# Gate_up in sections of two weight tiles, the scatter's halves between them, in a routed-expert loop

## The chip, the cores and the metric

One core of a Trainium2 chip runs the whole kernel. The metric is the device time of one execution in microseconds; lower is better. Before the change the median of 3 runs is 1408.82 us (1407.81 to 1412.9).

## What is computed

One encoder layer over 256 tokens of width 1024 in float32: an input projection feeds three mixers (latent attention, a Mamba-2 scan, a convolution module), gates merge them, an output projection and a layer norm follow. Then comes the part that matters here, a mixture of 32 experts with 4 experts per token, and a second layer norm:

```python
logits = (t @ router_w + router_b).astype(jnp.float32)
top_vals, top_idx = lax.top_k(logits, TOP_K)
gates = jax.nn.softmax(top_vals, axis=-1).astype(t.dtype)
...
h = xe @ w_gu[e] + b_gu[e]
gate, up = h[:, :D_FF], h[:, D_FF:]
gate = jnp.minimum(gate, SWIGLU_LIMIT)
up = jnp.clip(up, -SWIGLU_LIMIT, SWIGLU_LIMIT)
return ((up + 1) * (gate * jax.nn.sigmoid(SWIGLU_ALPHA * gate))) @ w_dn[e] + b_dn[e]
```

Each expert's rows are weighted by their gates and added to their tokens.

## The kernel before, in words

The program goes through the 32 experts in a fixed order. Each has 12 weight tiles of 1 MB (128 partitions by 2048 floats): tiles 0 to 7 are gate_up, each one slice of 128 of the 1024 inputs, tiles 8 to 11 are down. SP issues a load per tile, in order, into a ring of 19 slots; `load` waits until PE has read the slot's former tile for the last time. The first 19 tiles are loaded during the mixers.

How many tokens an expert has is known only at run time, so its code has conditional sections, entered or skipped by each engine. With up to 32 tokens (`size` 0) `up_four` runs: four matmuls for a tile, on four groups of 32 columns. With 33 to 64 (`size` 1) `up_many` runs instead, for 64 tokens. With 65 to 96 (`size` 2) both run, the first 64 tokens in one and the rest in the other. The down projection has the same two kinds of section. The router puts 84, 68 and 72 tokens on experts 2, 15 and 17; experts 3, 6, 7, 10, 12, 18, 24, 25, 30 and 31 have 33 to 64, all others no more than 32. No expert has over 96; for such experts there is an overflow loop, `heavy`, placed before expert 31 and guarded by one comparison of the largest count on PE, ACT, DVE and POOL. It is skipped here.

An expert's result is weighted (`weigh`, on ACT and DVE: yh, then yl) into tiles that all experts share (`parked`: sc, yh, yl). It is added to the tokens one expert later, by `flush(prev)`: for each half c of the tokens four matmuls (L1150) scatter it into two PSUM banks, and DVE adds both banks to the accumulator (L1154). The tag `sm` has two banks in all, so the second half's matmuls wait for the first half's adds. PE's order is the order in which the code is written. In `expert` it is: the sections of tiles 0 to 3, `flush(prev)`, then `aux` (the slots of the tokens and their gates, L1236 and L1097), then the sections of tiles 4 to 7, and then `fill` (part of a later expert's gather) and the down projection. Expert 31 is special: since `heavy` writes into `parked`, the scatter of expert 30 is done before the guard of the overflow loop.

The lines that the change touches:

```python
        for k0 in (0, KT // 2):
            with tc.If(pe > 0):
                up_many(k0)
            with tc.If(pe != 1):
                up_four(k0)
            if k0 == 0:
                flush(prev)
                aux = bank(5, f"aux{e}", [P, S + 2])
```

Of the kernel before, what the change touches and what calls it, by code (L numbers as in the profile page):

```python
# [10 lines left out]
F32R = mybir.dt.float32r  # L11
# [7 lines left out]
P = 128  # L19
D = 1024  # L20
S = 256
KT = D // P
# [155 lines left out]
def tile_trunk(ctx, tc, xT_d, xn_d, wf_d, vec_d, row_d, rw_d, cst_d, cst2_d, rope_d, ln1_d, ln2_d,  # L178
               bgu_d, bdn_d, wgu_d, wdn_d, out_d):
    nc = tc.nc  # L180
    V, A, T, PO = nc.vector, nc.scalar, nc.tensor, nc.gpsimd
# [539 lines left out]
    def load(e, u, n=None, eng=nc.sync):  # L721

        if (e, u) in pre:
            return pre.pop((e, u))
        t = ring_tile(f"{e}_{u}", n)
        if u < 8:
            eng.dma_start(t, wgu_v[e, u])
        else:
            t = t.rearrange("p (k n) -> p k n", k=2)
            eng.dma_start(t, wdn_v[e, (u - 8) // 2, u % 2])  # L730
        return t
# [424 lines left out]
    def flush(prev, cs=(0, 1)):  # L1156
        if prev:
            e, sc, yh, yl = prev
            for c in cs:
                pos = [sm(f"pos{e}{c}{n}") for n in range(2)]  # L1160
                scatter(pos, c, sc, (yh, yl))
                for n in range(2):
                    add(c, n, pos[n])
# [9 lines left out]
    def expert(e, oh, xg, bl, wt, prev, cur, fill):  # L1173
# [34 lines left out]
        def up_many(k0):  # L1208
            if k0 == 0:
                for q in range(2):  # L1210
                    T.matmul(pL[q], bl, bgu_t[:, q * 512:(q + 1) * 512], start=True, stop=False)
            for k in range(k0, k0 + KT // 2):
                for q in range(2):
                    for h in range(2):
                        T.matmul(pL[q][h * 64:(h + 1) * 64].rearrange("p (g n) -> p g n", g=2),  # L1215
                                 xg[:, k, s_], quarter(wt[k], h, q), start=False, stop=(k == KT - 1))

        def up_four(k0):
            if k0 == 0:
                for g, (h, q) in enumerate(QUARTERS):  # L1220
                    T.matmul(grp(pS, g), bl[:, g * TINY:(g + 1) * TINY].bitcast(F32),  # L1221
                             bgu_t[:, q * 512:(q + 1) * 512].bitcast(F32), start=True, stop=False)
            for k in range(k0, k0 + KT // 2):
                for g, (h, q) in enumerate(QUARTERS):
                    T.matmul(grp(pS, g).rearrange("p (g n) -> p g n", g=2), xs_[:, k],  # L1225
                             quarter(wt[k], h, q), start=False, stop=(k == KT - 1))

        for k0 in (0, KT // 2):
            with tc.If(pe > 0):
                up_many(k0)  # L1230
            with tc.If(pe != 1):
                up_four(k0)
            if k0 == 0:
                flush(prev)
                aux = bank(5, f"aux{e}", [P, S + 2])
                T.matmul(aux[:, 0:S], idr[:, e:e + 1].to_broadcast([P, P]), rankT, start=True, stop=True)  # L1236
                gate_mm(aux[:, S:S + 1], lambda c: oh[:, c, e % 2], e)
                gate_mm(aux[:, S + 1:S + 2], lambda c: ohs[:, c], e)
                gsl = ex.tile([P, 2], F32, tag="gsl", name=f"gsl{e}", bufs=4)
                V.tensor_copy(gsl, aux[:, S:S + 2])  # L1240
# [125 lines left out]
    prev = None  # L1366
    for e in range(NE):
        more = e // 2 + 1 < NE // 2
        if e % 2 == 0:
            oh, xg = ohn, xgn  # L1370
            if more:
                ohn = mo.tile([P, 2, 2, CAP], F32R, tag="ohp", name=f"ohp{e + 2}", bufs=2)
                xgn = mo.tile([P, KT, P], F32, tag="xg", name=f"xg{e + 2}", bufs=2)
                with tc.issue_after(last["ch"].ins):
                    for c in range(2):
                        onehot(ohn, c, e + 2)

        def fill(arm="", e=e, more=more):
            if more and e % 2 == 0:
                pg = [sm(f"pgx{e}{arm}{hf}") for hf in range(2)]  # L1380
                for c in range(2):
                    gather(pg, c, pair(ohn, c))
                A.copy(raw[:, 0:512], pg[0])
                V.tensor_copy(raw[:, 512:D], pg[1])
            elif more:
                spread_rows(xgn, rowk, f"{e}{arm}")

        wt = [load(e, u) for u in range(12)]
        bl = nbl
        if e + 1 < NE:  # L1390
            nbl = bias_lhs(e + 1)
        if e == NE - 1:

            flush(prev)
            prev = None
            free = [nload[0] + i for i in range(4)]
            with tc.If(count(NE, ALL) > TOP, label="overflow"):
                for x in range(NE):
                    with tc.If(count(x, ALL) > TOP):
                        for part in range(2):  # L1400
                            heavy(x, part, [load(x, u, free[u % 4], PO) for u in range(12)], (f"{x}x", *parked))
        cur = (e, *parked)
        with pe_order():
            expert(e, oh, xg, bl, wt, prev, cur, fill)
        prev = cur
# [153 lines left out]
```

## Time and profile before

| what | value |
|---|---|
| median of 3 runs | 1408.82 us |
| the profiled execution's own time | 1414.25 us |
| its span, first to last instruction | 1412.4 us |
| PE busy | 1169.7 us (83%) |
| DVE busy | 614.1 us (43%) |
| ACT busy | 328.1 us (23%) |
| transfers over the span | 322 GB/s on average |
| mean granted TensorE clock | 0.902 |
| matmul records of L1225 (`up_four`) and L1215 (`up_many`) | 1408 and 832 |

A section over one tile leaves 8 records, so 64 records are one expert: 22 experts ran `up_four` and 13 ran `up_many`. The mixers fill the span up to about 400 us, the experts take nearly all the rest, the last layer norm some 20 us. PE's share is an average over both parts; a matmul's end is modelled, so a busy PE may still be waiting in part. PEclk is the share of full clock that TensorE was granted. In a timeline row, the text in brackets is the idle time of the engine before the row and what ended it; a name with a q, as PEq, is an engine's sequencer, at the line of the section that it passed.

### The profile page before, as it was taken

What the parts mean: (1) busy time and instruction counts of PE and PEld (TensorE: products, weight loads), DVE (VectorE), ACT (ScalarE), POOL (GpSimd) and SP (SyncE); (2) the same over time, 40 slices, a digit from 0 to 9 for tenths busy, and PEclk for the clock granted to TensorE, in tenths of its full rate; (3) what the DMA queues carried; (4) which work ended last, traced back from release to release, by engine and by line L of the source; (5) the groups of instructions that cost most, each with busy time, mean ns of one, the idle gap of its engine ahead of it and who ended that gap; (6) DMA issues with size and microseconds to landing.
All of it is one profiled execution on the core that took longest, in us unless ns stands there. A gap on an engine that the chain in (4) does not pass through costs nothing. (4 is left out here: it accounts for less than half of the span.)

```text
span 1412.4 us, 20889 instructions
## 1 busy us (share of the span) xinstructions
PE 1169.7 (83%) x7635; PEld 620.8 (44%) x7635; DVE 614.1 (43%) x1245; ACT 328.1 (23%) x668; POOL 293.4 (21%) x293
## 2 busy tenths in 40 slices
PE   7797797899957987887888879898888888877875
PEld 7786687799822433233232324242322323212222
DVE  5999996877653233223323221323233322222213
ACT  5565563545421011101110010111001011000001
POOL 5999999543030000000000000000000000000000
PEclk9898888899968899999998998999989999987897
DMA  7342333467949878999999999997999999999991
GB/s 249 106 149 100 109 135 135 149 211 268 328 170 416 328 308 349 414 416 415 417 414 415 415 414 418 416 416 281 384 416 414 414 416 416 416 416 415 414 396 45
DMA packets 89496, 456.39 MB, mean 323 GB/s; under 512 B 8304, under 2 KB 8704, under 8 KB 58496
## 3 DMA queue, kind: packets, MB, share of 16 engines
q1 hardware_dynamic: 89344, 454.33, 81.3%
q8 instruction: 99, 1.62, 0.5%
q14 instruction: 53, 0.43, 0.1%
HBM read 453.25 MB, written 1.05 MB: 322 GB/s over the span
## 5 line engine op out<-in xcount | busy, mean ns | idle before, releaser
L1225 PE MATMUL pGS<-ew,xsm 128*32 128x512 f32 x1408 | 194.8, 694 | 23.8 <-DMA ew<-in_wgu_dram 12.1
L1448 POOL TENSOR_TENSOR xn<-xn,lb 128x256 f32<-128x256 f32 x4 | 2.8, 723 | 993.3 <-DVE xn L1436 993.3
L1215 PE MATMUL pGL<-ew,xg 128*64 128x512 f32 x832 | 203.3, 642 | 2.8 <-DMA ew<-in_wgu_dram 2.8
L1154 DVE TENSOR_TENSOR xn<-xn,pos 128x512 f32<-128x512 f32 x124 | 79.9, 684 | 221.2 <-PE pos L1150 218.8
L1143 DVE SCALAR_TENSOR_TENSOR yl<-pY,gsl,yh 128x512 fp32r<-128x512 f32 x35 | 26.3, 751 | 236.0 <-ACTq L1202 93.0
L1087 ACT ACTIVATE sg<-gv 128x256 f32<-128x256 f32 x48 | 20.0, 417 | 459.1 <-DVE gv L1086 458.3
L388 POOL TENSOR_TENSOR cbc<-cbc,ups 128x256 f32<-128x256 f32 x120 | 124.4, 1036 | 4.6
L1215 PEld LDWEIGHTS pGL<-ew,xg 128*64 128x64 f32 x832 | 66.2, 147 | 123.5 <-issue 112.1
L1225 PEld LDWEIGHTS pGS<-ew,xsm 128*32 128x32 f32 x1408 | 55.2, 123 | 141.9 <-issue 110.6
L243 DVE TENSOR_TENSOR wl<-raw,wh 128x1024 fp32r<-128x1024 f32 (+1 forms) x72 | 98.9, 1382 | 38.4 <-ACT wh L242 38.0
L1296 PE MATMUL pY<-ew,hT 128*32 128x512 f32 x704 | 91.3, 664 | 23.2 <-ACT hT L1282 21.9
L242 ACT CAST wh<-raw 128x1024 fp32r<-128x1024 f32 (+1 forms) x89 | 90.9, 1030 | 61.5 <-DMA raw<-in_wf_dram 20.5
L1265 PE MATMUL pY<-ew,hT 128*64 128x512 f32 x416 | 101.2, 643 | 0.0
L387 POOL TENSOR_TENSOR ups<-ups,vec 128x256 f32<-128x256 f32 x120 | 100.6, 857 | 0.0
L1150 PE MATMUL pos<-yh,sc 64*128 64x512 f32 x124 | 47.7, 513 | 31.9 <-DVE xn L1154 24.1
L1142 ACT ACTIVATE yh<-pY,gsl 128x512 fp32r<-128x512 f32 x35 | 24.1, 687 | 191.9 <-PE pY L1265 87.5
L1265 PEld LDWEIGHTS pY<-ew,hT 128*64 128x64 f32 x416 | 30.9, 147 | 61.5 <-issue 60.0
L1296 PEld LDWEIGHTS pY<-ew,hT 128*32 128x32 f32 x704 | 22.2, 120 | 77.7 <-issue 44.2
L1150 PEld LDWEIGHTS pos<-yh,sc 64*128 64x128 f32 x124 | 18.0, 189 | 83.5 <-DVE xn L1154 50.7
L1086 DVE TENSOR_SCALAR gv<-pGS 128x256 f32<-128x256 f32 x22 | 9.3, 425 | 103.7 <-PE pGS L1225 103.7
L1221 PE MATMUL pGS<-bgu_t,bl 128*32 128x512 f32 x176 | 24.3, 622 | 35.5 <-DVEq L1202 13.5
L243 POOL TENSOR_TENSOR wl<-raw,wh 128x1024 fp32r<-128x1024 f32 x17 | 41.6, 2451 | 52.6 <-ACT wh L242 52.6
(446 smaller groups left out, 2182.7 us busy)
## 6 DMA issues: line engine op xcount, KB each, us to landing
ew<-in_wgu_dram SPq DMA_DIRECT2D x241, 1024.0 KB, 19.9
ew<-in_wdn_dram SPq DMA_DIRECT2D x124, 1024.0 KB, 20.0
raw<-in_wf_dram SPq DMA_DIRECT2D x87, 512.0 KB, 3.9
ew<-in_wgu_dram SPq DMA_DIRECT2D x30, 512.0 KB, 7.0
ew<-in_wdn_dram SPq DMA_DIRECT2D x8, 512.0 KB, 5.2
xraw<-in_xT_dram SPq DMA_DIRECT2D x4, 256.0 KB, 5.4
xn<-in_xn_dram SPq DMA_DIRECT2D x2, 512.0 KB, 6.5
lnt<-in_ln_dram SPq DMA_DIRECT2D x2, 512.0 KB, 10.1
```

The source lines that it names most:

```text
L242: A.copy(h[:, b], raw[:, b])
L243: (PO if u in LOW_POOL else V).tensor_sub(l[:, b], raw[:, b], h[:, b].bitcast(F32))
L387: PO.tensor_tensor(pr, up[:, j:j + S], W("cw31", c * 31 + j).to_broadcast([P, S]), op=ALU.mult)
L388: PO.tensor_add(acc, acc, pr)
L1143: V.scalar_tensor_tensor(yl, pY, gsl, yh.bitcast(F32), op0=ALU.mult, op1=ALU.subtract)
L1150: T.matmul(pos[n], sc[r, c * P:(c + 1) * P], y[r], start=(start and i == 0), stop=(i == 1))
L1154: V.tensor_add(dst, dst, po)
L1215: T.matmul(pL[q][h * 64:(h + 1) * 64].rearrange("p (g n) -> p g n", g=2), xg[:, k, s_], quarter(wt[k], h, q), start=False, stop=(k == KT - 1))
L1221: T.matmul(grp(pS, g), bl[:, g * TINY:(g + 1) * TINY].bitcast(F32), bgu_t[:, q * 512:(q + 1) * 512].bitcast(F32), start=True, stop=False)
L1225: T.matmul(grp(pS, g).rearrange("p (g n) -> p g n", g=2), xs_[:, k], quarter(wt[k], h, q), start=False, stop=(k == KT - 1))
L1265: T.matmul(pY[0][n * 64:(n + 1) * 64], hT[b][:, j, h * CAP:(h + 1) * CAP], wt[KT + 2 * b + h][:, j, n * 512:(n + 1) * 512], start=False, s ...
L1296: T.matmul(grp(pY, 2 * n + j), hT[:, j, g * TINY:(g + 1) * TINY], w[:, j, n * 512:(n + 1) * 512], start=(j == 1 and (b, h) == (0, 0)), sto ...
```

## The change

The gate_up part runs in four pairs of sections of two tiles each instead of two pairs of four. The two halves of the scatter come after the first and the second pair, `aux` after the third. Before expert 31 the overflow loop no longer uses `parked`: it takes tiles of its own (`rest`, from the tags `ohp` and `xg`), so `flush(prev)` in front of it is gone, and expert 31 scatters expert 30's result like every other expert.

```diff
--- before.py
+++ after.py
@@ -1209,7 +1209,7 @@
             if k0 == 0:
                 for q in range(2):
                     T.matmul(pL[q], bl, bgu_t[:, q * 512:(q + 1) * 512], start=True, stop=False)
-            for k in range(k0, k0 + KT // 2):
+            for k in (k0, k0 + 1):
                 for q in range(2):
                     for h in range(2):
                         T.matmul(pL[q][h * 64:(h + 1) * 64].rearrange("p (g n) -> p g n", g=2),
@@ -1220,18 +1220,19 @@
                 for g, (h, q) in enumerate(QUARTERS):
                     T.matmul(grp(pS, g), bl[:, g * TINY:(g + 1) * TINY].bitcast(F32),
                              bgu_t[:, q * 512:(q + 1) * 512].bitcast(F32), start=True, stop=False)
-            for k in range(k0, k0 + KT // 2):
+            for k in (k0, k0 + 1):
                 for g, (h, q) in enumerate(QUARTERS):
                     T.matmul(grp(pS, g).rearrange("p (g n) -> p g n", g=2), xs_[:, k],
                              quarter(wt[k], h, q), start=False, stop=(k == KT - 1))
 
-        for k0 in (0, KT // 2):
+        for k0 in range(0, KT, 2):
             with tc.If(pe > 0):
                 up_many(k0)
             with tc.If(pe != 1):
                 up_four(k0)
-            if k0 == 0:
-                flush(prev)
+            if k0 <= 2:
+                flush(prev, (k0 // 2,))
+            elif k0 == 4:
                 aux = bank(5, f"aux{e}", [P, S + 2])
                 T.matmul(aux[:, 0:S], idr[:, e:e + 1].to_broadcast([P, P]), rankT, start=True, stop=True)
                 gate_mm(aux[:, S:S + 1], lambda c: oh[:, c, e % 2], e)
@@ -1391,14 +1392,14 @@
             nbl = bias_lhs(e + 1)
         if e == NE - 1:
 
-            flush(prev)
-            prev = None
+            rest = (mo.tile([P, S], F32R, tag="ohp", name="sch", bufs=2),
+                    *[t[:, i] for t in (mo.tile([P, 2, 512], F32R, tag="xg", name="yx", bufs=2),) for i in range(2)])
             free = [nload[0] + i for i in range(4)]
             with tc.If(count(NE, ALL) > TOP, label="overflow"):
                 for x in range(NE):
                     with tc.If(count(x, ALL) > TOP):
                         for part in range(2):
-                            heavy(x, part, [load(x, u, free[u % 4], PO) for u in range(12)], (f"{x}x", *parked))
+                            heavy(x, part, [load(x, u, free[u % 4], PO) for u in range(12)], (f"{x}x", *rest))
         cur = (e, *parked)
         with pe_order():
             expert(e, oh, xg, bl, wt, prev, cur, fill)
```

PE, expert 15, around the scatter, before (pos: the scatter's banks, aux: the slots' bank, pGS and pGL: the accumulators of the 32- and the 64-token kind, ew_15_3: weight tile 3 of expert 15):

```order
L1225 MATMUL pGS_9279<-ew_15_3_9196,xsm_9233 32x512 x4
L1231 UNCONDITIONAL_BRANCH x2
L1150 MATMUL pos_9320<-yh,sc 128x512
L1150 MATMUL pos_9321<-yh,sc 128x512
L1150 MATMUL pos_9320<-yl,sc 128x512
L1150 MATMUL pos_9321<-yl,sc 128x512
L1150 MATMUL pos_9328<-yh,sc 128x512
L1150 MATMUL pos_9329<-yh,sc 128x512
L1150 MATMUL pos_9328<-yl,sc 128x512
L1150 MATMUL pos_9329<-yl,sc 128x512
L1236 MATMUL aux_9336<-rankT,idr 128x256
```

There the whole scatter stands behind the section of tiles 0 to 3. PE, the same expert after the change, from weight tile 1 of the 32-token kind on:

```order
L1225 MATMUL pGS_9339<-ew_15_1_9252,xsm_9293 32x512 x4
L1231 UNCONDITIONAL_BRANCH x2
L1150 MATMUL pos_9364<-yh,sc 128x512
L1150 MATMUL pos_9365<-yh,sc 128x512
L1150 MATMUL pos_9364<-yl,sc 128x512
L1150 MATMUL pos_9365<-yl,sc 128x512
L1229 COMPARE_AND_BRANCH
```

Only the first half of the scatter is left there, behind the section of tiles 0 and 1. PE, the same expert after the change, a little further on, behind tiles 2 and 3 of the 64-token kind:

```order
L1231 COMPARE_AND_BRANCH
L1225 MATMUL pGS_9339<-ew_15_2_9254,xsm_9293 32x512 x4
L1225 MATMUL pGS_9339<-ew_15_3_9256,xsm_9293 32x512 x4
L1231 UNCONDITIONAL_BRANCH x2
L1150 MATMUL pos_9390<-yh,sc 128x512
L1150 MATMUL pos_9391<-yh,sc 128x512
```

The scatter's second half has moved behind the sections of tiles 2 and 3, and a pair of sections stands between the halves.

DVE before expert 31, up to the guard of the overflow loop (xn is the accumulator, cnt the counts), before:

```order
L1202 UNCONDITIONAL_BRANCH x2
L1154 TENSOR_TENSOR xn<-xn,pos_14260 128x512
L1154 TENSOR_TENSOR xn<-xn,pos_14261 128x512
L1154 TENSOR_TENSOR xn<-xn,pos_14268 128x512
L1154 TENSOR_TENSOR xn<-xn,pos_14269 128x512
L1362 TENSOR_LOAD cnt
L1397 COMPARE_AND_BRANCH
```

All four adds stand ahead of the guard. DVE behind the overflow loop, after the change:

```order
L1398 UNCONDITIONAL_BRANCH
L1229 UNCONDITIONAL_BRANCH
L1231 UNCONDITIONAL_BRANCH
L1154 TENSOR_TENSOR xn<-xn,pos_27697 128x512
L1154 TENSOR_TENSOR xn<-xn,pos_27698 128x512
```

The adds for expert 30 have moved from before the guard to behind it; the second two follow one pair of branches later, in the same way.

## Rows read from the trace of the kernel before

**Rows 1.** The page, GB/s moved by the transfers in 40 slices of the span.
```profile
GB/s 249 106 149 100 109 135 135 149 211 268 328 170 416 328 308 349 414 416 415 417 414 415 415 414 418 416 416 281 384 416 414 414 416 416 416 416 415 414 396 45
```

**Rows 2.** Stretches: us, busy PE PEld DVE ACT POOL, PEclk, DMA share, GB/s.
```profile
410.80:546.70 135.90, 119.06 (x724) 44.21 (x724) 37.91 (x93) 16.47 (x37) 1.58 (x1) 0.89 0.85 341
851.00:978.50 127.50, 114.90 (x690) 47.02 (x689) 34.24 (x85) 14.95 (x37) 0.00 (x0) 0.88 0.99 403
874.70:878.10 3.40, 3.40 (x16) 1.20 (x12) 1.16 (x6) 0.00 (x0) 0.00 (x0) 0.52 1.02 417
978.50:989.00 10.50, 8.44 (x56) 2.73 (x56) 4.67 (x8) 1.76 (x3) 0.00 (x0) 1.00 0.36 122
1017.40:1031.00 13.60, 10.23 (x89) 3.92 (x93) 4.44 (x11) 0.06 (x1) 0.00 (x0) 0.91 0.96 386
1031.00:1376.00 345.00, 276.40 (x1777) 96.14 (x1771) 90.68 (x212) 36.87 (x83) 0.00 (x0) 0.89 1.01 414
```

**Rows 3.** Waits of SP's queue: who on whom, us in total, times, longest.
```profile
SPq L730 <- DMA ew<-in_wgu_dram: 194.5, 94, 3.3
...
SPq L727 <- PE pGS L1225: 81.5, 33, 25.5
```

**Rows 4.** Timeline of SP at the ends of the two stalls: start us, us, line.
```profile
546.66 4.27 SPq L727 DMA_DIRECT2D ew<-in_wgu_dram  x5
...
984.30 11.15 SPq L727 DMA_DIRECT2D ew<-in_wgu_dram  x5
```

**Rows 5.** Timeline of PE, experts 30 and 31: start us, us, line, tiles, [idle before <-releaser].
```profile
1329.63 1.94 PE L1215 MATMUL pGL<-ew,xg 128*64 128x512 f32 x8 [0.56 <-DMA ew<-in_wgu_dram]
...
1335.51 8.78 PE L1215 MATMUL pGL<-ew,xg 128*64 128x512 f32 x32
...
1347.55 7.09 PE L1265 MATMUL pY<-ew,hT 128*64 128x512 f32 x32
1356.87 0.50 PE L1150 MATMUL pos<-yh,sc 64*128 64x512 f32 x2 [2.22 <-DVEq L1275]
...
1363.15 1.19 PE L1211 MATMUL pGL<-bgu_t,bl 128*128 128x512 f32 x2 [2.85 <-DVEq L1397]
```

**Rows 6.** Timeline of PE, expert 16.
```profile
913.91 0.51 PE L1150 MATMUL pos<-yh,sc 64*128 64x512 f32 x2
914.25 0.39 PE L1150 MATMUL pos<-yl,sc 64*128 64x512 f32 x2
915.42 1.09 PE L1150 MATMUL pos<-yh,sc 64*128 64x512 f32 x2 [0.78 <-DVE xn L1154]
...
916.68 0.39 PE L1236 MATMUL aux<-rankT,idr 128*128 128x256 f32 x1
...
918.14 3.64 PE L1225 MATMUL pGS<-ew,xsm 128*32 128x512 f32 x32 [0.51 <-PEq L1229]
```

**Rows 7.** Timeline of PE, expert 15.
```profile
871.02 0.50 PE L1150 MATMUL pos<-yh,sc 64*128 64x512 f32 x2
...
873.79 0.38 PE L1236 MATMUL aux<-rankT,idr 128*128 128x256 f32 x1
...
874.70 8.78 PE L1215 MATMUL pGL<-ew,xg 128*64 128x512 f32 x32
```

**Rows 8.** Timeline of DVE between experts 30 and 31.
```profile
1355.41 0.75 DVE L1143 SCALAR_TENSOR_TENSOR yl<-pY,gsl,yh 128x512 fp32r<-128x512 f32 x1 [8.15 <-ACT yh L1142]
1357.95 1.28 DVE L1154 TENSOR_TENSOR xn<-xn,pos 128x512 f32<-128x512 f32 x2 [1.79 <-DVEq L1202]
...
1360.34 0.69 DVE L1154 TENSOR_TENSOR xn<-xn,pos 128x512 f32<-128x512 f32 x1 [0.19 <-PE pos L1150]
```

**Rows 9.** Timeline of PE, expert 31's up projection.
```profile
1372.70 0.35 PE L1236 MATMUL aux<-rankT,idr 128*128 128x256 f32 x1 [0.31 <-PEq L1231]
...
1373.58 7.09 PE L1215 MATMUL pGL<-ew,xg 128*64 128x512 f32 x32
```

**Rows 10.** Timeline of DVE, expert 16.
```profile
921.83 0.42 DVE L1086 TENSOR_SCALAR gv<-pGS 128x256 f32<-128x256 f32 x1 [3.50 <-PE pGS L1225]
```

## The prediction

> **What bounds the kernel now.** I read the slices first, then the stretches, then who waits on SP, then PE expert by expert. From the middle of the span on the traffic line stands at 414 to 418 GB/s, with a few holes [rows 1]. That is the expert loop streaming its 1 MB weight tiles, and there it is bound by the transfers: 345 us long they ran at 414 GB/s, share 1.01 [rows 2]. One tile then takes 1.05 MB / 415 GB/s = 2.52 us, an expert of 12 tiles 30.3 us. SP's longest waits are on its own older transfers, 194.5 us, which is the healthy state; the unhealthy one is a wait for PE to give a tile's slot back, such as 81.5 us on the matmuls of L1225 [rows 3]. So PE's speed matters only where it holds slots back or is itself last. There are three such places.
>
> (a) The start. From 410.8 to 546.7 us (experts 0 to 3) PE is busy 119.06 of 135.90 us and the transfers have a share of 0.85 [rows 2]. The last starved load is issued at 546.66, when expert 3's down projection is over [rows 4]. Whatever PE gains before that instant moves the whole later stream.
>
> (b) Experts 15 to 18. Experts 15 and 17 run both the section for 64 tokens and the one for 32. PE is busy 114.90 of 127.50 us, then the transfers drop to a share of 0.36 for 10.5 us, until loads go out at 984.30, when expert 17's down tiles are free; the last small hole (0.96) ends with expert 18's [rows 2, 4].
>
> (c) The tail. Experts 29 and 30 are in step with the transfers again: two waits of PE in expert 30's first half are ended by a weight tile (one of them: 0.56 us) [rows 5]. But expert 31 starts late. PE ends expert 30's down at 1347.55 + 7.09 = 1354.64, then scatters it, then goes by the overflow guard (over 96 tokens?), and begins expert 31 at 1363.15 [rows 5], while at 2.52 us a tile from tile 3 of expert 30 (1329.63) tile 0 of expert 31 is there at about 1352.3, and the last of its 12 at about 1380. In the last slice the transfers move almost nothing, 45 GB/s [rows 1].
>
> **The change part by part.**
>
> *The scatter in two halves.* Today eight matmuls stand together. Expert 16: first at 913.91, the second four wait 0.78 us for DVE's adds to empty the two PSUM banks, aux starts at 916.68: 2.77 us [rows 6]. Expert 15 shows the same 2.77 us (871.02 to 873.79) [rows 7]. Two matmuls step 0.34 us on (913.91 to 914.25), so four cost 0.68 us and both halves 1.36, if the wait is gone. It is: the adds begin 1.08 us after the first matmul and take 1.28 us (1356.87, 1357.95) [rows 5, 8], so both banks are free 2.36 us after it, while the second half now comes at the earliest 0.68 us + a skipped section + two tiles of the 32-token kind (3.64 us for four [rows 6]) = 2.5 us plus the skip. **Gain 1.41 us** in each expert that has a scatter before it.
>
> *Two more pairs of sections.* In an expert that runs both kinds a taken section costs nothing: expert 15's scatter follows L1225 and the next L1215 follows aux without idle time [rows 7]. A skipped one costs 0.51 us where the 64-token kind is skipped [rows 6] and 0.31 us in the other case [rows 9]. I take 0.5 for all, so 1.0 us more per expert of one kind. The nearest rows lie there; the far bound is the skip of the overflow loop, 2.85 us [rows 5]; below, nothing. The Trainium skill, "Advanced Engine Details and Errata", Control Flow Timing, gives a compare-and-branch about 108 ns. By it, as an estimate, the twelve skips of the sum would cost 1.3 us and the sum would be -14.7 where the rows give -10.0; the measured gaps hold more than the branch, so the rows decide.
>
> *Earlier release of tiles* in experts that run the 64-token kind: no credit, since both stalls end on down tiles, whose section is unchanged [rows 4].
>
> *aux and its copy, two tiles later.* DVE idles 3.50 us before the clamp after them [rows 10]; two tiles take 1.8 of that. Free; without the cover DVE would delay the clamp. SP gets four more branches per expert between loads: hidden by the queue of older transfers, except at the two restarts, where I leave it to the range.
>
> *The overflow loop's own rows.* Expert 30's scatter no longer has to come before the guard. Today DVE's last add ends at 1360.34 + 0.69 = 1361.03 and PE starts 2.12 us later [rows 5, 8]. Now the guard waits for expert 30's weighing only: yl ends at 1356.16, 1.52 us after the down matmuls [rows 8].
>
> **The sum.**
> (a) Three scatters (experts 1, 2, 3) save 4.2; skips in experts 0, 1, 3 cost 3.0: -1.2 us.
> (b) Four scatters save 5.6; skips in 16 and 18 cost 2.0: -3.6 us.
> (c) Expert 30: scatter halves and aux fall into gaps between tiles. The up part today ends near 1344.3 (1335.51 + 8.78 [rows 5]). Tile 7 lands at about 1329.63 + 4 x 2.52 = 1339.7, and a tile takes 1.94 us [rows 5], so 1341.6 is the bound and the skips fit before it: 2.7 us earlier, down ends at 1351.9. Weighing +1.52 and guard +2.12: expert 31 begins at 1355.6 instead of 1363.15, 7.6 earlier. Inside it pays 1.36 for the scatter and 1.0 for skips: -5.2 us.
> Together -10.0, with twelve skips in it: six in (a), four in (b), two in (c).
>
> *TensorE's clock* is a separate term. In expert 15 the second four tiles take 8.78 us, in expert 31 7.09 for the same work [rows 7, 9]: after the scatter with its wait and the small matmuls of aux the granted clock is 0.52 of full speed from 874.7 to 878.1, the lower of its levels (1.2 instead of 2.4 GHz); the mean over (b) is 0.88 [rows 2]. Experts 2 and 17 repeat expert 15's row. With that sparse work cut into three pieces, each behind a dense section, I expect no fall there: 3 x 1.69 = 5.1 us (one in (a), two in (b)). Bounds: 0, and 6.8 if expert 1 gains as much.
>
> Total 15.1 us. The profiled execution took 1414.25 us, 5.4 above the median 1408.82; I take the same difference from both: 1399.1 for that one, **1393.7** for the median. Half a per cent, about what a measurement of this kernel can tell from no change, is 7.0 us.
>
> **Rivals.**
> 1. *The clock falls all the same* (expert 16 runs its next tiles in 3.64 us, without a fall, after the same scatter [rows 6], so the scatter alone does not decide it). Then -10.0: 1398.8.
> 2. *Only the tail gains.* The stalls (a) and (b) might end on something else than PE: the SP rows name transfers first [rows 3]. Against it: shares 0.85 and 0.36 beside a PE that is 88 and 90% busy [rows 2]. Then -5.2: 1403.6, no change.
> 3. *Slower: skips fetch.* Each of the 12 skips on the path could cost what the skip of the overflow loop does, 2.85 us with DVE's part in it [rows 5]. Without skips the sum is -10.0 - 6.0 = -16.0; 12 x 2.85 = 34.2 makes it +18.2: 1427.0. Break-even is 16.0 / 12 = 1.33 us a skip, and from 1.9 us on it is slower by 7 us. Against it: today's skips jump over twice as many matmuls for 0.31 to 0.51 us [rows 6, 9]. The Trainium skill, "Runtime: NRT & Kernel Launch", Instruction fetch mechanics, says that a taken branch to instructions outside the small window already loaded forces a fetch; it speaks for this rival, and the short gaps of these rows speak against its biting here.
> 4. *The second half still waits*, because DVE's adds come later than I think: up to 0.78 us back in each of seven experts, 5.5 us: 1399.2.
>
> **How the numbers follow.** Forecast (clock held, in some measure) 0.50; rivals 1 and 4 together 0.24; rival 2 0.16; rival 3 0.10. Lower end: skips at 0.31 (+2.3 us of gain), expert 1's clock (1.7), a faster start of expert 31 (1.2): 1388. Upper end: rival 2's time with skips at 0.73 us, that is 1406; above it lies rival 3 and little else. Faster by over 0.5% (below 1401.8): the forecast and rivals 1 and 4, less a little, 0.72. Within: rival 2, 0.19. Slower: 0.09.
>
> **What would show it.** In the profile after: no PE wait on DVE's add (L1154) before the second half; gaps of about 0.3 to 0.5 us at each skipped section; the second stall's loads (today 984.30) about 6 us earlier against the stream; expert 31's bias matmul some 7 us earlier against the last transfer; L1215 groups after aux at full clock in experts 2, 15, 17. The prediction is wrong if gaps at skips exceed 1.3 us, if the stalls end at other loads, or if the overflow guard before expert 31 takes as long as the scatter did.

## The result, and the profile after

| | kernel before | changed kernel |
|---|---|---|
| median of the runs, us | 1410.2 (1407.8 to 1412.9, 4 runs) | 1397.8 (1397.1 to 1398.0, 4 runs) |
| span of the profiled execution, us | 1412.4 | 1396.0 |
| mean granted clock of TensorE | 0.902 | 0.925 |

The ratio is 0.9911, 95% interval 0.989 to 0.9931: faster by 12.4 us, where 15.1 was forecast. The time lies inside the range (1388 to 1406). The two profiled executions differ by 16.4 us, more than the medians; why is said below.

The page of the changed kernel, GB/s in 40 slices; it answers to [rows 1].
```profile
GB/s 251 108 151 106 107 136 136 127 203 269 315 173 415 414 331 336 414 416 416 416 415 415 414 415 417 416 416 345 391 416 412 414 417 415 416 416 415 414 402 57
```
The same two holes, both shallower: 331 and 336 where 328, 308 and 349 stood (the first of these slices now has 414), 345 and 391 where 281 and 384 stood.

Stretches of the changed kernel, the columns as in [rows 2]: experts 0 to 3, the stretch up to the second stall, the stall, and from expert 30's last down matmul to expert 31's first tile.
```profile
410.90:538.75 127.85, 110.93 (x724) 39.77 (x724) 38.06 (x92) 16.29 (x37) 1.61 (x1) 0.95 0.90 362
843.00:960.00 117.00, 105.86 (x669) 40.48 (x670) 34.40 (x85) 14.90 (x36) 0.00 (x0) 0.90 1.02 416
960.00:970.40 10.40, 8.79 (x48) 2.80 (x48) 3.69 (x6) 1.07 (x2) 0.00 (x0) 0.97 0.60 249
1337.36:1346.91 9.55, 1.12 (x2) 0.50 (x2) 0.75 (x1) 0.69 (x1) 0.00 (x0) 0.61 1.01 413
```
The first stretch is 8 us shorter (135.90 before) and its clock rose from 0.89 to 0.95. The second stall carries 249 GB/s instead of 122. The last row is one that the forecast did not hold: 9.55 us in which PE does 1.12 us of work.

PE's waits over the whole span (who on whom: us in total, times, longest). The kernel before:
```profile
PE pos L1150 <- DVE xn L1154: 24.1, 31, 1.1
...
PE pGS L1225 <- PEq L1229: 8.7, 18, 0.6
```
The changed kernel:
```profile
PE pGS L1225 <- PEq L1229: 19.8, 40, 0.9
...
PE pGL L1211 <- DVEq L1398: 8.4, 1, 8.4
```
The scatter's wait for DVE's adds, 31 times, is gone. The waits behind a skipped section are up from 18 to 40, and the wait at the guard is 8.4 us long, where it was 2.85 us behind a scatter [rows 5].

PE's timeline, experts 15 and 16 of the changed kernel (start us, us, line, tiles, [idle before <-releaser]); it answers to [rows 6, 7].
```profile
862.23 0.50 PE L1150 MATMUL pos<-yh,sc 64*128 64x512 f32 x2
862.57 0.40 PE L1150 MATMUL pos<-yl,sc 64*128 64x512 f32 x2
...
868.33 0.38 PE L1237 MATMUL aux<-rankT,idr 128*128 128x256 f32 x1
...
869.24 3.65 PE L1215 MATMUL pGL<-ew,xg 128*64 128x512 f32 x16
...
902.62 1.93 PE L1225 MATMUL pGS<-ew,xsm 128*32 128x512 f32 x16 [0.46 <-PEq L1229]
```
In expert 15 the scatter's second half (862.23) follows without idle time, and the two tiles behind aux take 3.65 us, which is full clock; before, the four tiles behind aux took 8.78 us, 4.39 a pair [rows 7]. In expert 16 each half is followed by 0.46 us at the skipped section.

The restarts of SP's loads (start us, us, line), which answer to [rows 4]:
```profile
538.73 5.96 SPq L727 DMA_DIRECT2D ew<-in_wgu_dram  x5
...
970.40 2.90 SPq L727 DMA_DIRECT2D ew<-in_wgu_dram  x4
```
They are 7.9 and 13.9 us earlier. From there to the last landing the stream keeps its lead: the last tile lands at 1366.79 instead of 1381.36 us, 14.6 earlier.

Between experts 30 and 31, PE of the changed kernel, then expert 31's gate_up:
```profile
1345.79 1.20 PE L1211 MATMUL pGL<-bgu_t,bl 128*128 128x512 f32 x2 [8.43 <-DVEq L1398]
...
1352.24 0.66 PE L1150 MATMUL pos<-yh,sc 64*128 64x512 f32 x2 [0.31 <-PEq L1231]
...
1356.88 0.51 PE L1150 MATMUL pos<-yh,sc 64*128 64x512 f32 x2 [0.16 <-PEq L1231]
```
The branch and semaphore rows of the guard's line, all engines (op, count, duration in ns, first and last start), kernel before:
```profile
L1397 ACTq EVENT_SEMAPHORE  x2: 17/17/17, 1360.2 to 1360.3; - x2
...
L1397 DVEq EVENT_SEMAPHORE  x2: 21/21/21, 1363.0 to 1363.1; - x2
...
L1397 ACTq COMPARE_BRANCH  x1: 69/69/69, 1357.2 to 1357.2; - x1
...
L1397 DVEq COMPARE_BRANCH  x1: 85/85/85, 1361.0 to 1361.0; - x1
```
The changed kernel:
```profile
L1398 ACTq EVENT_SEMAPHORE  x2: 17/17/17, 1342.8 to 1342.8; - x2
L1398 DVEq EVENT_SEMAPHORE  x2: 21/21/21, 1345.6 to 1345.7; - x2
...
L1398 ACTq COMPARE_BRANCH  x1: 69/69/69, 1339.9 to 1339.9; - x1
L1398 DVEq COMPARE_BRANCH  x1: 91/91/91, 1341.3 to 1341.3; - x1
```
Each engine compares, jumps over the loop, and signals behind it; PE starts with the last signal. DVE's jump took 2.0 us before (1361.0 to 1363.0) and takes 4.3 now (1341.3 to 1345.6). Counted from expert 30's last down matmul (1354.64 and 1337.36) the compare is now 2.4 us earlier, the signal at the same point: 8.3 us. That is the part of the forecast that failed, and the first thing to test.

What DVE waits for there stands in the DMA records, which keep packets of instructions apart from the weights. In DVE's jump they hold one packet of 8 KB on queue 14 (queue, kind: packets, MB, share of 16 engines), first in the kernel before (1360.99 to 1362.99 us), then in the changed one (1341.31 to 1345.62):
```profile
q14 instruction: 1, 0.01, 1.0%
...
q14 instruction: 1, 0.01, 0.5%
```
The packet starts 6.40 and 6.32 us after expert 30's last down matmul, and DVE's signal follows it by 1.95 us in both. In the nine traces that have guard and hint in these places (before, changed, e1, e2 and e5 to e9 below) the packet starts at 6.25 to 6.42 us and the signal comes 1.93 to 1.98 us later, whether DVE's compare came at 3.9 or at 6.2 to 6.4 us. A packet of 16 KB on queue 8 stands near it too, but moves against the signal from run to run. So, as far as these rows tell, DVE waits for a load of the code behind the loop. Another packet on queue 14 starts 2.45 to 2.72 us earlier, and ACT's signal follows that one by some 1.7 us. Why the two are that far apart isn't shown; it is about the time of one weight tile (2.52 us in the forecast), but whether loads of code wait behind weights no run tests.

### The profile page after: what moved, and what is told of

Its sections match the earlier page's. It is cut to its first block, busy times and chain, and to the rows that moved or that the text cites. A ratio compares the mean times of both kernels' runs of the same rounds, so it can differ in the third digit from the quotient of the medians.

```text
span 1396.0 us, 21188 instructions
## 1 busy us (share of the span) xinstructions
PE 1135.2 (81%) x7635; PEld 590.5 (42%) x7635; DVE 613.3 (44%) x1245; ACT 328.7 (24%) x668; POOL 293.7 (21%) x293
## 5 line engine op out<-in xcount | busy, mean ns | idle before, releaser
L1225 PE MATMUL pGS<-ew,xsm 128*32 128x512 f32 x1408 | 191.7, 649 | 54.8 <-DMA ew<-in_wgu_dram 32.1
L1215 PE MATMUL pGL<-ew,xg 128*64 128x512 f32 x832 | 196.5, 611 | 2.5 <-DMA ew<-in_wgu_dram 2.0
L1225 PEld LDWEIGHTS pGS<-ew,xsm 128*32 128x32 f32 x1408 | 44.5, 114 | 161.0 <-issue 104.5
L1297 PE MATMUL pY<-ew,hT 128*32 128x512 f32 x704 | 84.6, 613 | 27.0 <-ACT hT L1283 20.2
L1215 PEld LDWEIGHTS pGL<-ew,xg 128*64 128x64 f32 x832 | 57.2, 140 | 111.8 <-issue 91.4
L1221 PE MATMUL pGS<-bgu_t,bl 128*32 128x512 f32 x176 | 27.9, 705 | 35.6 <-DVEq L1202 10.7
L1188 ACT COPY xsm<-xg 128x256 f32<-128x256 f32 x32 | 12.9, 402 | 134.9 <-PE pGS L1225 124.5
L1150 PEld LDWEIGHTS pos<-yh,sc 64*128 64x128 f32 x124 | 12.5, 186 | 58.7 <-issue 58.6
```

Source lines behind the costliest of these rows:

```text
L1297: T.matmul(grp(pY, 2 * n + j), hT[:, j, g * TINY:(g + 1) * TINY], w[:, j, n * 512:(n + 1) * 512], start=(j == 1 and (b, h) == (0, 0)), sto ...
```

## The experiments

Twelve kernels ran, each beside the kernel before on its chip. The kernel before had medians of 1409.8 to 1412.2 us there, in runs from 1402 to 1418, so ratios are compared, and where one or two us matter, the trace. The last columns are from the traces: expert 30's last down matmul to expert 31's first tile; expert 31's end after the last landing; gate_up of expert 18.

| kernel | median us | ratio to before, 95% | gap 30 to 31 | end after landing | gate_up 18 |
|---|---|---|---|---|---|
| before | 1410.2 | 1 | 9.63 | 11.25 | 18.11 |
| changed | 1397.8 | 0.9911 (0.989 to 0.9931) | 9.55 | 9.51 | 17.68 |
| e1_kept | 1399.1 | 0.9933 (0.9908 to 0.9958) | 9.62 | 8.54 | 17.59 |
| e2_rows_only | 1414.5 | 1.0034 (1.0 to 1.0067) | 9.61 | 16.69 | 18.12 |
| e3_no_loop | 1390.1 | 0.9868 (0.9818 to 0.9917) | 2.72 | 2.64 | 17.60 |
| e4_early_guard | 1392.0 | 0.9895 (0.9848 to 0.9942) | 2.71 | 4.46 | 17.69 |
| e5_whole | 1421.2 | 1.0081 (1.0047 to 1.0115) | 9.58 | 18.15 | 21.07 |
| e6_whole_aux | 1434.0 | 1.0141 (1.01 to 1.0181) | 9.47 | 17.71 | 22.56 |
| e7_split4 | 1406.3 | 0.997 (0.9946 to 0.9993) | 9.64 | 8.52 | 16.05 |
| e8_one_tile | 1432.2 | 1.0141 (1.0099 to 1.0184) | 9.49 | 13.07 | 20.27 |
| e9_three | 1395.7 | 0.9898 (0.9879 to 0.9917) | 9.64 | 12.11 | 17.09 |
| e10_no_hint | 1398.1 | 0.9902 (0.9877 to 0.9926) | 11.27 | 11.25 | 17.60 |
| e11_best | 1386.8 | 0.9831 (0.9813 to 0.9849) | 2.79 | 4.29 | 17.10 |
| e12_hint29 | 1399.1 | 0.992 (0.9895 to 0.9946) | 10.14 | 11.41 | 17.68 |

### What is the overflow guard worth?

**e1_kept.** Part 3 of the change undone.
```diff
-            rest = (...)
+            flush(prev)
+            prev = None
...
-    heavy(x, part, [...], (f"{x}x", *rest))
+    heavy(x, part, [...], (f"{x}x", *parked))
```


> The changed kernel, but with the scatter of expert 30 back before the guard (part 3 of the change undone). Theory A (the vector engine's way over the overflow loop takes so long that the scatter before the guard costs nothing): expert 31's first gate_up matmul still comes 9.5 us (9.0 to 10.0) after expert 30's last down matmul, expert 31's gate_up loses the scatter and is 2.4 us shorter, so 1395.4 us, between 1394.5 and 1398. Theory B (the forecast's: the guard is worth 2.1 us and the rest of the wait was the scatter): the gap grows by the scatter, and the tail is 5 us longer: 1403 us, 1401.5 to 1404.5.

The gap is 9.62 us, theory A's. The scatter before the guard cost nothing: PE in this kernel, as the row of the gap before had it:
```profile
1341.99 0.50 PE L1150 MATMUL pos<-yh,sc 64*128 64x512 f32 x2 [2.23 <-DVEq L1276]
...
1348.26 1.19 PE L1211 MATMUL pGL<-bgu_t,bl 128*128 128x512 f32 x2 [2.83 <-DVEq L1398]
```
DVE's signal comes 8.3 us after the down matmuls here too, with the compare at 6.4 us instead of 3.95. Expert 31's gate_up fell by 1.2 us (18.95 to 17.72), half of what theory A took off. The time, 1399.1, is above A's band and its interval does not exclude B's 1403; the decision is the trace's.

**e2_rows_only.** Part 3 alone, on the kernel before.
```diff
-            flush(prev)
-            prev = None
+            rest = (...)
...
-    heavy(x, part, [...], (f"{x}x", *parked))
+    heavy(x, part, [...], (f"{x}x", *rest))
```


> The kernel before, with part 3 alone (rows of its own for the loop, expert 30's scatter inside expert 31, sections of four weight tiles). Theory A: the gap before expert 31 stays near 9.6 us, and expert 31's gate_up gets a whole scatter with its wait of about 1.4 us for the vector engine, so 2 to 4 us slower than before: 1412 to 1414 against 1410.2. Theory B: the gap falls to about 2 to 3 us, the scatter is paid inside: 5 us faster than before, 1405 (1403.5 to 1407).

1.0034, with an interval that begins at 1: no gain, which is A and not B. Expert 31 ends 16.69 us after the last landing (11.25 before). The whole scatter now stands in its gate_up, and the gate_up's last four tiles run at a granted clock of 0.73: 9.70 us, where 7.09 stood before [rows 9].
```profile
1366.91:1376.61 9.70, 9.70 (x39) 2.80 (x32) 0.90 (x3) 0.19 (x1) 0.00 (x0) 0.73 0.10 40
```

**e3_no_loop.** The loop, its guard and its hint taken out. (The hint is a marker in expert 30's down section that tells PE, ACT and DVE of the overflow branch as likely taken.)
```diff
-            with tc.If(count(NE, ALL) > TOP, label="overflow"):
...
-            tc.mark_branch_hint_location("overflow", ...)
```


> The changed kernel without the overflow loop, its guard and its hint (it leaves out what experts with over 96 tokens would need; none has so many here). Theory A: the guard costs the tail all of its 7 to 8 us: expert 31's first gate_up matmul comes 1 to 2 us after expert 30's last down matmul, the weight stream bounds expert 31, its last down matmul ends 2 us after the last landing, and the kernel is 7.5 us faster: 1390.3 (1389 to 1392). Theory B: the guard itself is worth only 2.1 us, the rest of the wait lies on other work (weighing, loads of registers): 1395.7 (1394.5 to 1397).

1390.1 us. PE's row of expert 31's start:
```profile
1339.36 0.70 PE L1209 MATMUL pGL<-bgu_t,bl 128*128 128x512 f32 x2 [2.09 <-DVEq L1274]
```
The gap falls by 6.8 us to 2.72, and expert 31 ends 2.64 us after the last landing. So the guard was worth 6.9 us of the tail (9.51 to 2.64), not 2.1, and the time is theory A's. That the stream then bounds expert 31, as A had it, is not in the trace: PE waits there at skips and for DVE, 0.2 to 1.1 us each, and for no weight tile.

**e4_early_guard.** The guard, with a scatter ahead of it, to before expert 28, where PE waits for weights anyway.
```diff
-        if e == NE - 1:
+        if e == NE - 4:
...
-            rest = (...)
+            flush(prev)
+            prev = None
```
(The hint moves with it, and the loop takes the parked rows again.)

> The changed kernel with the overflow loop, its guard and hint, and a scatter ahead of it, moved from before expert 31 to before expert 28, where the tensor engine waits for weights for about 10 us in each of two experts. Theory A: the guard's 7 to 9 us lie beside that wait, expert 28 catches up with the stream, expert 31 follows expert 30 at once, 7.5 us faster: 1390.3 (1389 to 1392.5). Theory B: the guard is worth only 2.1 us of the tail: 1395 to 1396. Theory C: the wait before expert 28 holds ring slots so that the loads start late and the tail keeps the delay: 1397 to 1403.

The gap is 2.71 us, as without the loop, and the median 1392.0: A. DVE's jump takes 0.8 us here, as a packet of code on queue 14 starts 4.6 us after expert 27's last down matmul and its compare comes only at 5.8. Expert 30 ended 3.3 us later against the stream than in the changed kernel, so 4.46 us stay behind the last landing instead of 2.64. Of these 3.3 us 1.7 are expert 30's down matmuls, which took 8.79 us in this execution and 7.09 in the changed kernel's; whether the rest is theory C's is not shown.

**e10_no_hint.** The hint alone taken out.
```diff
-            tc.mark_branch_hint_location("overflow", hint="LikelyTaken", ...)
+            pass
```


> The changed kernel without the branch hint ahead of the guard. Theory A (the vector engine's jump over the loop ends 8.3 us after expert 30's last down matmul whether its compare came at 3.95 us or at 6.35 us, so the code behind the loop is on its way before the compare, and the hint starts that): without it the jump ends later, 1.5 to 4 us after 8.3 us, and the kernel is 1.5 to 4 us slower than the changed one. Theory B (the hint does nothing; the way to that code begins elsewhere): expert 31's first gate_up matmul stays 9.5 us (9.2 to 10) after expert 30's last down matmul, and the time within 1 us of the changed kernel's ratio of 0.991.

The gap grows by 1.72 us to 11.27. The rows of the guard's line in this run:
```profile
L1396 ACTq EVENT_SEMAPHORE  x2: 17/17/17, 1343.7 to 1343.8; - x2
...
L1396 DVEq EVENT_SEMAPHORE  x2: 21/21/21, 1346.3 to 1346.4; - x2
...
L1396 ACTq COMPARE_BRANCH  x1: 45/45/45, 1338.2 to 1338.2; - x1
...
L1396 DVEq COMPARE_BRANCH  x1: 62/62/62, 1339.9 to 1339.9; - x1
```
Unhinted, the jump takes 5.5 us on ACT and 6.4 on DVE; with the hint 2.9 and 4.3. A packet of code on queue 14 starts 8.03 us after the down matmuls, and DVE's signal follows by 1.96 us as before. So the time is in the way to the code behind the loop, which a hint shortens and does not hide. The gap is theory A's; its premise, that the code is on its way before the compare, is not borne out: in the changed kernel no packet of queue 14 starts between the hint (1329.38 us on DVE) and the first compare (1339.9). The kernel's time (0.9902) can't tell 1.7 us.

**e12_hint29.** The hint one expert earlier.
```diff
-        if e == NE - 2:
+        if e == NE - 3:
```


> The changed kernel with the branch hint one expert earlier, in expert 29's down section. Theory A (the hint starts the way to the code behind the loop, and 12 us before the compare are only too few): with 40 us the jump ends soon after the compare, expert 31's first gate_up matmul comes 5 to 6 us after expert 30's last down matmul in place of 9.55, and the kernel is 3.5 to 4.5 us faster than the changed one. Theory B (the branches of the skips in between, about ten on each engine, put the hinted code out again, or it waits for them): 11.3 us as without a hint, 1.7 us slower. Theory C (the hint acts only from the last skip on): 9.5 us as now.

None of the three. ACT's jump is over in 0.5 us, DVE's takes 4.9 us, and the gap is 10.14:
```profile
L1398 ACTq EVENT_SEMAPHORE  x2: 17/17/17, 1338.5 to 1338.6; - x2
...
L1398 DVEq EVENT_SEMAPHORE  x2: 21/21/21, 1344.6 to 1344.7; - x2
...
L1398 ACTq COMPARE_BRANCH  x1: 69/69/69, 1338.0 to 1338.0; - x1
...
L1398 DVEq COMPARE_BRANCH  x1: 91/91/91, 1339.7 to 1339.7; - x1
```
For ACT theory A holds (time was missing), for DVE it does not. Between the hints (1298 us) and the compares queue 14 carried one packet of code (1308.16 us), not one for each of the two; its next packets start 2.1 and 2.6 us after DVE's compare. Why DVE's hinted code comes so late is open; no run tells it.

### What are the sections, the split and the aux block worth?

**e5_whole.** Sections of two tiles, but the whole scatter in one place.
```diff
-            if k0 <= 2:
-                flush(prev, (k0 // 2,))
+            if k0 == 0:
+                flush(prev)
```


> The changed kernel with the whole scatter after the first pair of weight tiles (sections of two tiles and the aux block after the third pair stay). Theory A (the forecast's terms: the second half's wait for the vector engine costs 1.41 us in each of the 8 experts that bound the time: 1, 2, 3, 15 to 18 and 31): 8 x 1.41 = 11 us slower than the changed kernel, 1409 (1405 to 1412). Theory B (the gain is nearly all the tensor engine's clock, kept by the distance of the scatter from the aux block): within 3 us of the changed kernel's 1397.8.

1.0081, slower than the kernel before and 23 us above the changed one: both theories fell, A by half. The traced execution (1416.2 us) is the fastest of its seven and 18 us above the changed kernel's; 8.6 of these come behind the last landing (18.15 us instead of 9.51). PE in expert 18:
```profile
985.90 1.09 PE L1150 MATMUL pos<-yh,sc 64*128 64x512 f32 x2 [0.74 <-DVE xn L1154]
986.51 0.73 PE L1150 MATMUL pos<-yl,sc 64*128 64x512 f32 x2
987.16 5.35 PE L1215 MATMUL pGL<-ew,xg 128*64 128x512 f32 x16
993.05 3.65 PE L1215 MATMUL pGL<-ew,xg 128*64 128x512 f32 x16 [0.54 <-PEq L1231]
```
and the granted clock of the first group of tiles behind the scatter:
```profile
987.16:992.51 5.35, 5.35 (x17) 0.68 1.00 414
```
The 0.74 us wait is back, and the two tiles behind it run at 0.68: 5.35 us instead of 3.65. In the kernel before, the same scatter with the same wait in the same expert stood behind 7.09 us of matmuls at full clock and was followed by 7.09 us at full clock:
```profile
987.90 7.09 PE L1215 MATMUL pGL<-ew,xg 128*64 128x512 f32 x32
...
998.93 7.09 PE L1215 MATMUL pGL<-ew,xg 128*64 128x512 f32 x32
```
So here the wait costs 1.41 us, and 1.70 us of clock on top; gate_up of expert 18 is 3.4 us longer than in the changed kernel. It is the same in expert 3. In experts 1, 2 and 15 to 17 of this run the tiles behind the same scatter stay at full clock, though in the kernel before it was in experts 1, 2, 15 and 17 that they fell. The aux block, two sections away, has no part in it.

**e6_whole_aux.** The same, with the aux block right behind the scatter.
```diff
-            elif k0 == 4:
                 aux = bank(5, f"aux{e}", [P, S + 2])
```


> As the run before, and the aux block right behind the scatter, as in the kernel before; only the sections of two tiles and part 3 are left of the change. Theory A: 11 us of waits as in the run before, and the clock term of 5.1 us on top: 1414 (1410 to 1418), slower than the kernel before, since two more skips of 0.5 us in each of the 8 experts are all that is left. Theory B (clock alone): all of the gain goes, 1408 to 1412. Theory C (the clock falls or holds by the execution, not by this distance): as e5_whole, within 2 us.

1434 us, above all theories, and 13 us above the run before where the clock term had 5. The row shows the same group at a clock of 0.57:
```profile
1007.52:1013.85 6.33, 6.33 (x23) 1.71 (x16) 0.57 (x3) 0.00 (x0) 0.00 (x0) 0.57 0.79 321
```
6.33 us: another 1.0 us of clock in this expert. But theory A had its clock term in experts 2, 15 and 17, and there the tiles behind aux run at full clock, as in expert 15:
```profile
881.91 3.65 PE L1215 MATMUL pGL<-ew,xg 128*64 128x512 f32 x16
```
The loss is in experts 1, 3, 16 and 18 instead. So A's sum of terms fell, in size and in place; where all of the 13 us lie was not followed.

**e7_split4.** Four-tile sections, scatter halves after each.
```diff
+            flush(prev, (k0 // 4,))
             if k0 == 0:
-                flush(prev)
```


> The kernel before with the scatter's first half after the first section of four tiles and its second half after the second section (sections and the place of the overflow loop's rows as before). Theory A (waits of the scatter 1.41 us in each of 7 experts, none of the new skips; the second half lies beside the tensor engine's wait for SwiGLU): 1410.2 - 7 x 1.41 = 1400 (1396 to 1404), as good as the changed kernel without its sections. Rival (the second half delays the transposes and the vector engine's SwiGLU behind its adds): no gain or worse, 1408 to 1416.

0.997: 4.7 us faster, between the two. Expert 18's gate_up is 2.1 us shorter (16.05), aux right behind one half of the scatter costs no clock (7.09 us for the four tiles after it, in experts 2, 15 and 17 too, where the kernel before took 8.78; the first row below is expert 15), but the second half comes back in what follows (second row, expert 18):
```profile
868.68 7.09 PE L1215 MATMUL pGL<-ew,xg 128*64 128x512 f32 x32
...
995.76 1.10 PE L963 MATMUL pgx<-nh,ohp 128*128 128x512 f32 x2 [2.22 <-DVE xn L1154]
```
The next gather waits 2.22 us for DVE's adds, a delay of the rival's kind at another place, and in experts 3, 16 and 18 gate_up's end to down's end grows by more than was saved. The gain is in the experts that run both kinds (expert 17 ends its down 3.5 us sooner after its start).

**e8_one_tile.** Sections of one tile, scatter and aux at the same places.
```diff
-        for k0 in range(0, KT, 2):
+        for k0 in range(KT):
...
-            if k0 <= 2:
+            if k0 in (1, 3):
...
```


> The changed kernel with sections of one weight tile: eight pairs of branches in each expert, scatter halves and aux at the same places. Theory A (a skip costs 0.5 us of the tensor engine): 4 more skips in each of the 8 experts, 16 us slower than the changed kernel: 1414 (1409 to 1418). Rival (a skip costs 0.11 us, as the Trainium skill's page Advanced Engine Details and Errata, Control Flow Timing, would have it): 3.5 us slower, 1401 (1399 to 1404).

Four more skips make expert 18's gate_up 2.6 us longer (17.68 to 20.27) and expert 16's 2.7 (11.28 to 14.00): **0.65 to 0.68 us a skip**, a little above theory A's 0.5, six times the rival's 0.11. PE between two such sections:
```profile
990.23 1.94 PE L1215 MATMUL pGL<-ew,xg 128*64 128x512 f32 x8 [0.54 <-PEq L1231]
...
995.50 1.94 PE L1215 MATMUL pGL<-ew,xg 128*64 128x512 f32 x8 [0.43 <-PEq L1231]
```
0.43 to 0.54 us is idle; and two sections of one tile take 2 x 1.94 us, 0.23 more than one of two (3.65). The median lies above both theories. The profiled execution took 1417.7 us, as A had it, and another 1421.7; the other four of the six took 1431 to 1436.5 us, which no trace here covers: that stays open.

**e9_three.** Three sections of 3, 3 and 2 tiles; scatter half, then half and aux.
```diff
-        for k0 in range(0, KT, 2):
+        for k0 in range(0, KT, 3):
...
-            if k0 <= 2:
-                flush(prev, (k0 // 2,))
-            elif k0 == 4:
+            if k0 == 0:
+                flush(prev, (0,))
+            elif k0 == 3:
+                flush(prev, (1,))
```


> The changed kernel with three sections of 3, 3 and 2 weight tiles in place of four of two: the scatter's first half after the first, its second half and the aux block after the second. Theory A (a skip without work in its shade costs 0.4 to 0.7 us, as the runs with sections of one tile showed): gate_up of one size 0.4 to 0.7 us shorter than in the changed kernel (17.66 to about 17.2 in expert 18, 11.28 to about 10.8 in expert 16), so 3 to 5 us over the 8 experts: a ratio to the kernel before of 0.988 (0.985 to 0.991). Theory B (the second half with the aux block right behind it slows the tensor engine's clock, as in the run with whole scatter and aux block together): 1.7 us more in each of those experts, a ratio of 0.999 (0.996 to 1.003).

Gate_up of expert 18 is 17.09, of expert 16 10.76 us: 0.6 and 0.5 less, theory A. The second half and aux together cost no clock:
```profile
980.73 0.50 PE L1150 MATMUL pos<-yh,sc 64*128 64x512 f32 x2 [0.16 <-PEq L1231]
...
982.30 3.65 PE L1215 MATMUL pGL<-ew,xg 128*64 128x512 f32 x16
```
0.9898; the last landing is 2.9 us earlier than in the changed kernel, but this execution gave 2.6 back at the end. The median lies 2 us below the changed kernel's, which the intervals don't separate.

**e11_best.** Three sections and the guard before expert 27.
```diff
-        for k0 in range(0, KT, 2):
+        for k0 in range(0, KT, 3):
...
-        if e == NE - 1:
+        if e == NE - 5:
```
(The rest as in e9_three and e4_early_guard.)

> Three sections as in e9_three, and the overflow loop with its guard, hint and a scatter ahead moved to before expert 27. Theory A (both gains add: 7 us of the guard on the tail, 3 to 5 us of skips): 10 to 12 us faster than the changed kernel, a ratio to the kernel before of 0.983 (0.979 to 0.986). Rival (the guard before expert 27 delays experts 27 to 29 so that expert 30 starts late, as a part of it did before expert 28): half of the guard's gain, a ratio of 0.986 to 0.989.

0.9831, 1386.8 us: theory A, and 11 us below the changed kernel, with intervals that don't touch. The gap before expert 31 is 2.79 us. Its end is 4.29 us behind the last landing, so 1.7 us against e3_no_loop's 2.64 are still there.

## Why the prediction was right or wrong

**The split of the scatter (1.41 us an expert): right.** The wait on DVE's adds is gone. In expert 18 gate_up fell by 0.44 us (18.11 to 17.68), where 1.41 less two skips of 0.5 makes 0.41; in expert 16 it fell by 0.16 (11.44 to 11.28). With short sections the split can be worth more than its term: 3.4 us in expert 18 of e5_whole, where the clock fell behind the wait.

**The skips (0.5 us): right to a little too cheap.** With 1.41 for the split, these two experts leave 0.49 and 0.63 us a skip; e8_one_tile, with nothing between two sections, gives 0.65 to 0.68. Rival 3, that skips fetch at 2.85 us, is out; its rule (a taken branch to code not at hand waits for a fetch: the Trainium skill, "Runtime: NRT & Kernel Launch", Instruction fetch mechanics) fits the trace where the loop is skipped, 4.3 us on DVE, and not the near skips. The 0.11 us of "Advanced Engine Details and Errata", Control Flow Timing (also the Trainium skill), are not what a skip costs PE here.

**The stalls (a) and (b) with the clock (-9.9 us): right.** The restart of the second stall, counted from expert 0's first gate_up matmul, is at 573.5 and 563.9 us in the two executions with four-tile sections and undivided scatter (before, e2_rows_only), and at 556.2 to 561.1, mean 558.7, in the six with the change's sections (changed, e1, e3, e4, e10, e12). The difference of the means is 10.0, of which 1.9 had come by the first stall's restart (2.9 forecast) and 8.1 came after it (7.0 forecast). That it meets the sum so closely is in part luck: one mean rests on two executions 9.6 us apart. Of one pair of profiles it is 14.0, too much: the same early code spreads by 6.5 us by the first restart (127.8 to 134.3). The first tiles of expert 2's gate_up and expert 1's down run at full clock in some executions and not in others (gate_up 24.9 us or 26.6 to 26.8; down 3.64 us or up to 6.35), and the change doesn't decide it: expert 1's down took 6.25 us in the kernel before, 3.64 in e2_rows_only with the same early code, 3.64 in the changed kernel and 6.34 in e1_kept.

The clock term itself is real. The four tiles behind aux took 8.6 to 8.8 us in experts 2, 15 and 17 in both executions with the scatter undivided in long sections, and the two behind aux take 3.65 us in all six with the change's sections. Expert 1, left at the upper bound, gained too. Its four tiles behind aux took 5.34 us in both executions of the first kind, here the kernel before:
```profile
441.19 5.34 PE L1225 MATMUL pGS<-ew,xsm 128*32 128x512 f32 x32 [0.58 <-DMA ew<-in_wgu_dram]
```
In all six of the second kind a pair takes 1.92 us there, full clock. So the term of 5.1 us would have been nearer to its bound of 6.8. The reason that the forecast gave, sparse work in pieces, agrees with e7_split4, where only the scatter is divided. That this is needed is not shown: in e6_whole_aux, with short sections and with scatter and aux in one piece, experts 2, 15 and 17 kept their clock and others lost it.

**The tail (-5.2 us): wrong in one term.** Against the last landing it gained 11.25 - 9.51 = 1.74 us. Expert 30's down did end 2.7 us earlier against the stream, as forecast, and expert 31's gate_up grew by 2.55 us (2.36 forecast). The step that failed is "weighing +1.52 and guard +2.12": PE started 8.43 us after the down matmuls, not 3.64. The 2.12 us had been read behind DVE's last add, as if the guard began there. It was only what was left of DVE's wait for the code behind the loop; the adds before it were cover, not cost. The text named this as a sign that it is wrong ("if the overflow guard before expert 31 takes as long as the scatter did"). Expert 31's down, at full clock now, gave 1.5 us that no term held; without them the tail would have given 0.2.

With 1.74 in place of 5.2 the forecast's sum is 11.6 us, and 13.3 with expert 1's clock; 12.4 was measured, inside the range although the tail's mechanism was wrong. Rival 1 (clock) and rival 4 (second half still waits) are out by the rows; rival 2 had the places upside down: the stalls carried the gain, and the tail little.

## What to carry to other kernels

A wait that ends with a signal from another engine's branch is not shortened by taking away the work ahead of that branch, until the branch's own way is known: take the time from the last thing both versions share, not from the last work seen. A rarely taken loop belongs where an engine waits for memory anyway: with the same three sections, moving the guard from before the last expert to before expert 27 cut the gap before the last expert from 9.64 to 2.79 us and the time from 1395.7 to 1386.8 (e9_three, e11_best). And a short wait between dense stretches should be priced with what the clock does after it: in expert 18 of e5_whole the undivided scatter cost 3.4 us, of which the forecast's term for the wait holds 1.4.

## What the runs showed of the hardware that was not expected

- Jumping far over a loop that isn't taken (one trace each): 6.4 us on DVE and 5.5 on ACT without a hint, 4.3 and 2.9 with it some 12 us ahead; one expert earlier, ACT's falls to 0.5 and DVE's stays at 4.9. DVE's signal comes 1.93 to 1.98 us after a packet of code starts in nine traces, and its jump took 2.0 us where the compare came just before that packet.
- In experts 3 and 18 the same scatter with the same wait is followed by a granted clock of 0.68 behind 3.65 us of dense matmuls and of 1.00 behind 7.09 us of them. It is no rule: in experts 2, 15 and 17, which run both kinds, it is the other way round, up to 8.78 us for the next four tiles with long sections and full clock with short ones.
- The mean clock says little of the time: sections of one tile have the highest (0.950) and are among the slowest.
